# A hybrid attention and delta-rule layer on one core: fewer warm-up products ahead of the norm, a planner that counts a halved clock, and a new table of shifts

## The chip, the cores and the metric

The program runs on one core of one Trainium2 chip. The metric is device time in microseconds (us) of one execution; the time before is 871.31 us, the median of three runs. The engines are named as in the profile: PE is TensorE (its weight loads are PEld), DVE is VectorE, ACT is ScalarE, POOL is GpSimd, SP is SyncE, which issues nearly all transfers (its queue is SPq).

## What is computed

The reference is one layer over 512 latent tokens `x` of width 1024, with 256 context tokens `ctx`. Cut to what matters here:

```
mod = silu(c) @ w_ada + b_ada                       # and the same for c_ctx
h   = rms_norm(x,   g1) * (1 + sc1)  + sh1
hc  = rms_norm(ctx, g1) * (1 + csc1) + csh1
q, k, v, dq, dk, dv, dz, da, db, ga, gd = split(h @ w_in)     # and of hc @ w_in
y_attn = windowed attention with context keys, normed q and k, rotary positions, sinks
o_d    = gated delta rule in chunks of 64, forwards and backwards
y = sigmoid(ga) * (y_attn @ w_br_attn) + sigmoid(gd) * (y_d @ w_br_dn)
x = x + gt1 * (y @ w_out)
out = x + gt2 * (relu(norm(x) @ w_mlp1)**2 @ w_mlp2)
```

## The kernel before, in words

Features lie on the 128 partitions in eight groups of 128 (`kt` 0 to 7), tokens lie along the free axis. Every large product is made of three products in a rounded 32-bit format: the upper part of the weights by the upper and by the lower part of the features, and the lower part of the weights by the upper part of the features (`mm3`, L331, L333, L335). Upper parts are written by ACT, the lower ones by DVE. A weight tile takes one load, one ACT pass (L295) and one DVE pass (L300).

**The front.** PE begins with `NONES` = 30 products of a tile of ones by itself whose result nobody reads (L230). `norm_x` squares `x` in four pieces as they land (ACT L402, DVE L404 and L405) and sums them over the partitions with four products (L406); ACT then makes the inverse root of them (L185, a logarithm and an exponential). The condition vector goes through a SiLU on ACT (L185 on `c_cc`), which needs another table of functions than the logarithm, so a table load (L181) stands between the two. For each `kt`, `ada` brings two transfers of `w_ada` (512 KB each) and multiplies them in one group of eight L249; `columns` turns the result into columns (ACT L267, two PE L272, DVE L281 and L282); `features` and `features_c` make the upper and the lower part of `h` for `x` and for the context (DVE L339, ACT L340, DVE L341). Three weight tiles are worked on while this goes on: the one for `da` and `db` (`wab`) and two of `dk`. Unread products stand after the first columns (L276, eight of them) and after later ones (L434, fourteen in all). After them come the other tiles of `w_in` (`wh`, `wl`).

**The order of the work.** The order on each engine is not that of the code. `Lists` plays the whole program through with a table of costs (`Step.cost`): each instruction has a time in which its engine is taken and a time after which its result is there. Of the instructions that are ready on an engine, the one with the lowest rank goes next; the rank is the place in the code plus what the table `SHIFTS` adds for stretches of it. The order that comes out is then imposed on each engine. So a change of a cost or of a row of `SHIFTS` can move instructions anywhere in the program.

Further places that are spoken of: L566 in `qk_norm` sums the squares of `q` and `k` (ACT L563 makes the squares). L725 transposes attention weights, L894 and L1243 are small products of the delta rule, L1148 are products of the gates. At the end of the delta rule sixteen transposes (L1444) bring its result back to features on the partitions, DVE L1449 multiplies it by the gate, ACT L224 and DVE L225 split it, and the branch products (L331 again) read it. The output projection and the two MLP products follow.

Of the kernel before, what the change touches and what calls it, by code (L numbers as in the profile page):

```python
# [26 lines left out]
LEAD = 0  # L27
ATT = 32
NHALF = 3
NONES, NWAIT = 30, 8  # L30
AHEAD = 2
LATES = 3, 3
HPAUSE = 2
# [3 lines left out]
STICK = 50  # L37
NSKIP = 2
WARM = (0, 3, 3, 3, 2, 0, 0, 0)
NROWS = 2  # L40
ND1 = 3
NGD = 5
P = 128
# [8 lines left out]
HC = CH // 2  # L52
# [65 lines left out]
def tile_layer(ctx: ExitStack, tc: tile.TileContext, I: dict, out: bass.AP, dbg=None):  # L118
    nc = tc.nc
    V, A, G, PE = nc.vector, nc.scalar, nc.gpsimd, nc.tensor  # L120
# [17 lines left out]
    banks = Arena(lambda o, n: psum[:, o:o + n], 512, 8)  # L138
# [55 lines left out]
    ones = mats.tile([P, P], F32, name="ones")  # L194
# [33 lines left out]
    wb_ = banks.get(512, True)  # L228
# [166 lines left out]

    def norm_x():
        ss = bank()
        for i in range(4):
            b = alloc(1024)
            src = xs_[:, i * 1024:(i + 1) * 1024]  # L400
            n = 512 if i == 3 else 1024
            A.activation(b[:, :n], src[:, :n], AF.Square)  # L402
            if i == 3:
                V.tensor_tensor(b[:, n:], src[:, n:], src[:, n:], op=ALU.mult)  # L404
            V.tensor_tensor(b[:, :512], b[:, :512], b[:, 512:], op=ALU.add)  # L405
            PE.matmul(ss.ap, ones, b[:, :512], start=(i == 0), stop=(i == 3))  # L406
            b.free()
        act(rx, ss.ap, AF.Ln, bias=epsc, scale=1.0 / D)
        ss.free()
        return act(rx, rx, AF.Exp, scale=-0.5)  # L410
# [177 lines left out]
    own = [slice(0, 64), slice(64, 128)]  # L588
# [1163 lines left out]
class Step:  # L1752
# [39 lines left out]
    def cost(self):  # L1792

        n = self.cols
        if self.kind == "InstMatmult":
            if self.dtype.endswith("32r"):
                return (226 if n == 512 else max(60, 7 + .44 * n)), n * .44 + 175
            if self.dtype.endswith("16"):
                return 96, 240
            if self.whole:  # L1800
                return (110, 280) if self.ins.is_transpose else (max(62, 1.72 * n), max(62, 1.72 * n) + 170)
            return (142, 300) if self.tile[0] == P else (30 if self.tile[1] > HC else 19, 220)
        if self.kind == "InstStreamTranspose":
            return 1950, 2090
        if self.eng == "DVE":
            own = 67 + 1.04 * n + 60 * self.psum if n > 8 else 100
            return own, own + 85
        if self.eng == "Activation":
            own = 1290 if "Load" in self.kind else max(195, 36 + .893 * n) + 20 * self.psum
            return own, own + 130  # L1810
        return 550, 560
# [69 lines left out]
class Lists:  # L1881
# [27 lines left out]
    def run(self, rank):  # L1909

        n, after, gang, eng = self.n, self.after, self.gang, self.eng
        left, ready = list(self.left), [0.] * len(self.left)
        wait = [len(m) for m in self.members]
        free, links = [0., 0., 0., 0., 750.], [0., 0., 0., 0., 3200.]
        coming, here, out = [[] for _ in free], [[] for _ in free], []
        flight, whole, cold = [], True, False
        words, asked, begun, last = 0, {n: 0. for n in range(3)}, [0.] * n, 0.
        push, pop = heapq.heappush, heapq.heappop
        note = [SEEN[e] for e in self.ENGINES]

        def go(k):
            if k >= n:
                for x in after[k]:
                    ready[x] = max(ready[x], ready[k])
                    left[x] -= 1
                    if not left[x]:
                        go(x)
            elif gang[k] is None:
                push(coming[eng[k]], (ready[k], rank[k], k))
            else:  # L1930
                g = gang[k]
                wait[g] -= 1
                if not wait[g]:
                    t = max(ready[x] for x in self.members[g])
                    for x in self.members[g]:
                        push(coming[0], (t, rank[self.members[g][0]], x))

        for k in [k for k, m in enumerate(left) if not m]:
            go(k)
        for _ in range(n):  # L1940
            t, e = min((free[e] if here[e] else max(free[e], coming[e][0][0]), e) for e in range(5) if here[e] or coming[e])
            mine, come = here[e], coming[e]
            while come and come[0][0] <= t:
                push(mine, pop(come)[1:])
            k = mine[0][1]
            if e == 0 and self.whole[k] != whole:
                same = min((x for x in mine if self.whole[x[1]] == whole), default=None)
                if same and same[0] <= mine[0][0] + STICK:
                    k = same[1]
                    mine.remove(same)  # L1950
                    heapq.heapify(mine)
                else:
                    pop(mine)
            else:
                pop(mine)
            out.append(k)
            if self.dma[k]:
                if e == 4:
                    if len(flight) >= 8:
                        t = max(t, flight[-8])  # L1960
                    links[e] = end = max(t + (2400 if self.bytes[k] > 100000 else 1600), links[e]) + self.bytes[k] / 422
                    flight.append(end)
                    free[e] = t + 400
                else:
                    links[e] = end = max(t + 2400, links[e]) + self.bytes[k] / 159
                    free[e] = t + 900
            else:
                own, lag = self.cost[k]
                if e == 0:
                    words, had = words + self.words[k], words  # L1970
                    block = int(words / 256 + .63)
                    if block > int(had / 256 + .63):
                        asked[block] = max(t + 1100, links[4] - 500) + 1250
                    t = max(t, asked.get(int(had / 256 - .54), 0))
                    if self.whole[k] != whole:
                        t += 92 if whole else 130
                        cold = whole = self.whole[k]
                    elif cold and whole and self.wide[k]:
                        t, cold = t + 100, False
                end = t + lag  # L1980
                free[e] = t + own
            begun[k], last = t, max(last, end)
            for x in after[k]:
                if x >= n:
                    at = end + 40
                elif eng[x] == e and not self.dma[k]:
                    at = free[e] if e == 0 else end + 10
                else:
                    at = end + note[eng[x]]
                if at > ready[x]:  # L1990
                    ready[x] = at
                left[x] -= 1
                if not left[x]:
                    go(x)
        return out, begun, last


SHIFTS = (
# [12 lines left out]
)  # L2011


# [120 lines left out]
```

## Time and profile before

| what | value |
|---|---|
| median of three runs | 871.31 us (870.93 to 871.32) |
| profiled execution | 871.5 us, of which 869.7 us are its span |
| PE busy | 852.3 us, 98% of the span, 7544 products |
| DVE, ACT, POOL busy | 647.0, 498.4 and 26.1 us |
| granted TensorE clock, mean over the span | 1.00 |
| moved by DMA | 106.86 MB, 123 GB/s on average |
| SPq's transfers | 97.33 MB, 33.6% of the 16 DMA engines' span |

The span runs from the first to the last instruction; 1.8 us of the profiled execution lie around it. An engine counts as busy between the start and the modelled end of an instruction, and products overlap, so the time that one product takes from PE is read from the distance between starts. The first grant of the clock is not in the clock's column, which shows 1.00 from the start; what the clock was there is read from the distance of the products.

### The profile page before, as it was taken

The page shows a single profiled execution, that of the slowest core. Times are in us where ns is not written, and L with a number is a line of the kernel's source. Part 1 is how long each engine was busy: PE and PEld are TensorE (multiplying, and loading weights), DVE is VectorE, ACT ScalarE, POOL GpSimd, SP SyncE. Part 2 cuts the span into 40 slices and gives each one's busy share as a digit, 9 for nine tenths or more (in the row PEclk, how much of TensorE's full clock was granted, in tenths as well). Part 3 has the DMA queues.
Part 4 walks back from the last instruction along what each step waited for, and adds up shares of the span by engine and source line. Part 5 has one row for each costly group of instructions (what it writes and reads, how often), then busy time and mean ns, then how long its engine had stood idle before and what let it go on. Part 6 is the DMA issues. An engine that isn't in the chain of part 4 may idle for free.

```text
span 869.7 us, 17973 instructions
## 1 busy us (share of the span) xinstructions
PE 852.3 (98%) x7544; PEld 712.8 (82%) x7544; DVE 647.0 (74%) x1113; ACT 498.4 (57%) x882; POOL 26.1 (3%) x42
## 2 busy tenths in 40 slices
PE   9999999999999999899999999999999999999998
PEld 6688778877777778677778899888998899889986
DVE  4865899987779997867848969993876478648741
ACT  5567875487669886587754435552555256415620
POOL 0000001010000002000000000000000000000000
PEclk9999999999999999999999999999999999999999
DMA  9924465533121236733116744743412332342031
GB/s 365 352 72 98 88 134 122 120 76 70 38 38 31 68 131 212 243 99 100 40 54 220 264 144 131 249 139 121 146 33 74 122 140 70 97 128 92 26 121 49
DMA packets 31986, 106.86 MB, mean 123 GB/s; under 512 B 4001, under 2 KB 4513, under 8 KB 31905
## 3 DMA queue, kind: packets, MB, share of 16 engines
q1 hardware_dynamic: 29600, 97.33, 33.6%
q0 software_dynamic: 2304, 8.39, 6.2%
q8 instruction: 59, 0.97, 0.5%
q14 instruction: 23, 0.18, 0.1%
HBM read 103.61 MB, written 2.10 MB: 122 GB/s over the span
## 4 chain that ended last, share of the span: by engine, by line
PE 77%; DVE 9%; ACT 6%; DMA 6%; issue 2%; SPq 0%; ACTq 0%; DVEq 0%
PE banks L331 14%; PE banks L333 14%; PE banks L335 14%; PE banks L1612 14%; PE banks L1148 7%; DMA m<-in_wada 3%; PE banks L1243 3%; PE banks L1194 3%; ACT m L185 2%; PE banks L725 1%; DVE wl L300 1%; DMA wr<-in_win 1%; PE banks L781 1%; DVE m L511 1%; DMA wr<-in_wbr 1%
## 5 line engine op out<-in xcount | busy, mean ns | idle before, releaser
L331 PE MATMUL banks<-m,wh 128*128 128x512 f32 (+1 forms) x568 | 210.7, 374 | 2.2 <-ACT m L224 1.3
L333 PE MATMUL banks<-m,wh 128*128 128x512 f32 (+1 forms) x568 | 211.2, 372 | 0.0
L335 PE MATMUL banks<-m,wl 128*128 128x512 f32 (+1 forms) x568 | 209.9, 370 | 0.1
L295 ACT ACTIVATE wh<-wr 128x1024 fp32r<-128x1024 f32 (+1 forms) x92 | 90.4, 984 | 128.3 <-PE banks L333 82.7
L331 PEld LDWEIGHTS banks<-m,wh 128*128 128x128 f32 x568 | 107.0, 189 | 20.4 <-ACT m L224 1.5
L1612 PEld LDWEIGHTS banks<-m,m 128*128 128x128 f32 x1008 | 122.2, 192 | 0.7
L335 PEld LDWEIGHTS banks<-m,wl 128*128 128x128 f32 x568 | 106.9, 188 | 19.2 <-issue 1.0
L1612 PE MATMUL banks<-m,m 128*128 128x256 f32 x1008 | 122.4, 283 | 0.0
L333 PEld LDWEIGHTS banks<-m,wh 128*128 128x128 f32 x568 | 107.1, 188 | 18.1 <-issue 0.7
L224 ACT ACTIVATE m<-m 128x512 fp32r<-128x512 f32 (+2 forms) x118 | 82.4, 721 | 66.1 <-PE banks L1612 14.9
L1148 PE MATMUL banks<-m,wh 128*128 128x512 f32 x320 | 104.1, 402 | 1.8 <-ACT m L185 1.0
L225 DVE TENSOR_TENSOR m<-m,m 128x512 fp32r<-128x512 f32 (+2 forms) x118 | 92.3, 804 | 15.5 <-ACT m L224 13.9
L300 DVE TENSOR_TENSOR wl<-wr,wh 128x1024 fp32r<-128x1024 f32 (+1 forms) x76 | 84.3, 1109 | 17.1 <-ACT wh L295 14.6
L1739 DVE SCALAR_TENSOR_TENSOR m<-banks,modT,m 128x512 f32<-128x512 f32 x32 | 24.0, 749 | 65.0 <-PE banks L335 64.9
L1148 PEld LDWEIGHTS banks<-m,wh 128*128 128x128 f32 x320 | 58.6, 188 | 14.4 <-ACT m L185 1.4
L1148 PE MATMUL banks<-m,wl 128*128 128x512 f32 x160 | 63.7, 400 | 0.4 <-DVE wl L300 0.4
L331 PE MATMUL banks<-m,m 128*128 128x256 f32 (+1 forms) x136 | 45.5, 340 | 0.4 <-ACT m L295 0.3
L333 PE MATMUL banks<-m,m 128*128 128x256 f32 (+1 forms) x136 | 45.6, 342 | 0.1
L511 DVE SCALAR_TENSOR_TENSOR m<-m,m 128x1024 f32<-128x1024 f32 x32 | 39.1, 1222 | 8.4 <-DMA m<-in_wada 8.2
L335 PE MATMUL banks<-m,m 128*128 128x256 f32 (+1 forms) x120 | 40.2, 337 | 0.0
L1243 PEld LDWEIGHTS banks<-m,m 64*64 64x64 f32 x1600 | 26.7, 134 | 12.5 <-issue 4.3
L1148 PEld LDWEIGHTS banks<-m,wl 128*128 128x128 f32 x160 | 30.0, 188 | 7.3 <-DVE wl L300 1.1
(263 smaller groups left out, 1313.7 us busy)
## 6 DMA issues: line engine op xcount, KB each, us to landing
m<-in_wada SPq DMA_DIRECT2D x48, 512.0 KB, 4.8
wr<-in_wm SPq DMA_DIRECT2D x40, 512.0 KB, 3.6
wr<-in_win SPq DMA_DIRECT2D x38, 512.0 KB, 3.7
m<-in_wm SPq DMA_DIRECT2D x24, 512.0 KB, 3.7
wl<-in_win POOLq DMA_DIRECT2D x16, 512.0 KB, 5.8
m<-in_xT SPq DMA_DIRECT2D x8, 512.0 KB, 5.9
wr<-in_wbr SPq DMA_DIRECT2D x16, 256.0 KB, 2.7
wr<-in_wout SPq DMA_DIRECT2D x8, 512.0 KB, 4.4
```

Source lines behind the costliest of these rows:

```text
L224: A.activation(r32(hi), src, AF.Copy)
L225: (eng or V).tensor_tensor(r32(lo), src, hi, op=ALU.subtract)
L295: upper[0] = A.activation(r32(hi), raw, AF.Copy)
L300: V.tensor_tensor(r32(lo), raw, hi, op=ALU.subtract)
L331: PE.matmul(acc, w[0][:, k, :], xhi, start=(start and i == 0), stop=False)
L333: r = PE.matmul(acc, w[0][:, k, :], xlo, start=False, stop=(end and w[1] is None))
L335: r = PE.matmul(acc, w[1][:, k, :], xhi, start=False, stop=end)
L511: r = V.scalar_tensor_tensor(wa.ap, wa.ap, 0.5, scr_[0].ap, op0=ALU.mult, op1=ALU.mult, accum_out=modT[:, grp, j:j + 1])
L1148: PE.matmul(acc.ap, w[x][:, k, :], hx[k][y], start=(k == p == 0), stop=(k == KT - 1 and p == 2))
L1194: PE.matmul(pa.ap, w[x][:, j, :], r32(Q[y][:, :, j, :]), start=(j == p == 0), stop=(j == 3 and p == 2))
L1243: runs[n].append(PE.matmul(out_, w, x, start=True, stop=True).ins.name)
L1612: PE.matmul(dst, r32(self.w[w][i][:, k * P:(k + 1) * P]), xs7[x][k][j], start=(n == 0), stop=(n == 11))
```

## The change

The thirty unread products in front become sixteen. Inside `norm_x` four unread products follow the second of the four sums over squares and two follow the third (`XWARM`). In the planner a product that starts before 5500 ns takes twice its time (`COLD`), the costs of some kinds of products are changed, and an instruction that follows a transfer's issue on the same engine no longer waits for that transfer's end. The 60 rows of `SHIFTS` are replaced by 65 others.

```
-NONES, NWAIT = 30, 8
+NONES, NWAIT = 16, 8
+XWARM = (0, 4, 2, 0)
+COLD = 5500
...
         ss = bank()
+        wb_ = banks.get(512, True)
         for i in range(4):
...
-            PE.matmul(ss.ap, ones, b[:, :512], start=(i == 0), stop=(i == 3))
+            pe = PE.matmul(ss.ap, ones, b[:, :512], start=(i == 0), stop=(i == 3))
             b.free()
+            for _ in range(XWARM[i]):
+                follow(PE.matmul(wb_[:, :P], ones, ones, start=True, stop=True), pe)
+        wb_.free()
...
             if self.dtype.endswith("16"):
-                return 96, 240
+                return 80, 240
+            if self.whole and not self.ins.is_transpose:
+                return (max(224, 1.33 * n), max(224, 1.72 * n) + 170)
             if self.whole:
-                return (110, 280) if self.ins.is_transpose else (max(62, 1.72 * n), max(62, 1.72 * n) + 170)
-            return (142, 300) if self.tile[0] == P else (30 if self.tile[1] > HC else 19, 220)
+                return 110, 280
+            return (108, 400) if self.tile[0] == P else (30 if self.tile[1] > HC else 19, 220)
...
                 if e == 0:
+                    if t < COLD:
+                        own, lag = 2 * own, lag + own
...
                 elif eng[x] == e and not self.dma[k]:
                     at = free[e] if e == 0 else end + 10
+                elif eng[x] == e and self.dma[x]:
+                    at = free[e]
                 else:
...
 SHIFTS = (
-    (0, 2729, 2759, -37), (0, 7350, 8025, -10), (-1, 4917, 4924, 10), (0, 1436, 2436, 180), (-1, 5117, 5177, 30),
...
+    (-1, 5285, 5325, 5), (2, 2849, 2879, 1500), (0, 4631, 4781, 112), (-1, 7751, 7811, 1000), (-1, 2143, 2158, -90),
...
```

The rows of the table tell a reader nothing; what they do is seen in the order of the instructions. Lines of the changed kernel have other numbers (L148 becomes L150, L260 L262, L290 L292, L331 to L335 become L333 to L337, L566 L572, L894 L900, L918 and L919 L924 and L925, L1148 L1154, L1444 L1450), and buffers' numbers are some lower there. The small products of the delta rule keep their kinds; counted over the whole program, PE goes from whole-array products to products on a part of it or back 112 times before and 116 times now.

The first place is SP at the very start: `c_cc` is the condition vector, `c_prm` a table of small parameters, `in_wada` the weights of the modulation, `in_win` those of the input projection. Before:

```order
L260 DMA m_123<-in_xT 128x1024 x4
L148 DMA m_131<-in_wada 128x1024
L148 DMA m_137<-in_wada 128x1024
L148 DMA c_cc<-in_cc 128x16
L148 DMA c_prm<-in_prm 128x188
L309 DMA wr_143<-in_wab 128x512
L348 DMA m_124<-in_ctxT 128x1024 x2
L148 DMA m_153<-in_wada 128x1024
L148 DMA m_159<-in_wada 128x1024
L148 DMA m_221<-in_wada 128x1024
```

Now:

```order
L150 DMA c_cc<-in_cc 128x16
L150 DMA c_prm<-in_prm 128x188
L262 DMA m_109<-in_xT 128x1024 x4
L150 DMA m_117<-in_wada 128x1024
L150 DMA m_123<-in_wada 128x1024
L311 DMA wr_129<-in_wab 128x512
L350 DMA m_110<-in_ctxT 128x1024 x2
L150 DMA m_139<-in_wada 128x1024
L150 DMA m_145<-in_wada 128x1024
L292 DMA wr_153<-in_win 128x1024
L150 DMA m_213<-in_wada 128x1024
```

The two small transfers go ahead of `x`. The first tile of `w_in` goes ahead of the third pair of `w_ada` where it stood behind the first half of the fourth, and the second tile, which stood just ahead of the very last piece of `w_ada`, now stands ahead of the fifth pair.

The second place is PE between 104 and 114 us, in the middle of the first attention tiles (`m_1082` before and `m_1074` now hold the same squares, and so do `m_1188` and `m_1180`). Before:

```order
L894 MATMUL banks<-m_606 32x2x32 x4
L894 MATMUL banks<-m_608 32x2x32 x3
L566 MATMUL banks<-m_1082,c_bones 128x512
L333 MATMUL banks<-m_151,wh_817 128x512
L335 MATMUL banks<-m_151,wl_818 128x512
L331 MATMUL banks<-m_151,wh_817 128x512
```

Now:

```order
L333 MATMUL banks<-m_137,wh_809 128x512
L335 MATMUL banks<-m_137,wh_809 128x512
L337 MATMUL banks<-m_137,wl_810 128x512
L333 MATMUL banks<-m_137,wh_809 128x512
L572 MATMUL banks<-m_1074,c_bones 128x512
L335 MATMUL banks<-m_137,wh_809 128x512
L924 MATMUL banks<-m_1138,m_551 128x512
L925 MATMUL banks<-m_1138,m_551 128x512
```

Since the last sum of the kind before it, at 95 us, 28 wide (512) weight products came ahead of the first of the two, and now 46 and two more of L924 do. Counted from the same place, the second has 82 wide products ahead of it where it had 64, and the third, which follows right behind the second now, 82 where it had 90.

The third place is PE at 453 us, where the transposes of the delta rule's result (L1444, now L1450) stand between the last gate products (L1148, now L1154) and the first branch products. Before:

```order
L1148 MATMUL banks<-m_151,wl_5283 128x512
L1148 MATMUL banks<-m_151,wl_5407 128x512
L1148 MATMUL banks<-m_151,wh_5406 128x512 x2
L1148 MATMUL banks<-m_151,wl_5407 128x512
L1444 MATMUL banks<-c_ident,m_5369 128x128 x16
L331 MATMUL banks<-m_5362,wh_5439 128x512
```

Now:

```order
L1450 MATMUL banks<-c_ident,m_5361 128x128 x7
L1154 MATMUL banks<-m_137,wh_5398 128x512
L1450 MATMUL banks<-c_ident,m_5361 128x128
L1154 MATMUL banks<-m_137,wh_5398 128x512
L1154 MATMUL banks<-m_137,wl_5399 128x512
L1154 MATMUL banks<-m_137,wh_5398 128x512 x2
L1154 MATMUL banks<-m_137,wl_5399 128x512
L1450 MATMUL banks<-c_ident,m_5361 128x128 x5
L333 MATMUL banks<-m_5354,wh_5431 128x512
L1450 MATMUL banks<-c_ident,m_5361 128x128 x3
```

The first eight transposes went ahead of six gate products, and three of the last eight behind the first branch product. On ACT the first two splits (L224) of that result now stand ahead of the table load that they followed before.

## Rows read from the trace of the kernel before

**Rows 1.** Busy time in stretches of the span (stretch: its length, engines' busy us, clock, DMA).

```profile
44.00:72.00 28.00, 28.00 (x161) 24.51 (x160) 15.44 (x26) 19.22 (x26) 1.01 (x1) 1.00 0.28 79
72.00:460.00 388.00, 377.52 (x4675) 297.79 (x4674) 319.19 (x602) 277.45 (x576) 23.38 (x35) 1.00 0.38 99
460.00:869.70 409.70, 405.70 (x2391) 360.98 (x2389) 283.44 (x420) 175.91 (x238) 0.00 (x0) 1.00 0.38 123
```

**Rows 2.** Timeline of PE, first 13 us (start, us, what, idle before and releaser).

```profile
1.06 8.43 PE L230 MATMUL banks<-ones 128*128 128x128 f32 x60 [1.06 <-DVE ones L195]
9.33 3.60 PE L406 MATMUL banks<-m,ones 128*128 128x512 f32 x8
```

**Rows 3.** Busy time of L230 alone (PE, PEld), up to 4.16 us and after.

```profile
1.06:4.16 3.10, 3.10 (x14) 3.10 (x15) 1.00 0.74 243
4.16:9.33 5.17, 5.17 (x48) 5.14 (x46) 1.00 1.00 395
```

**Rows 4.** Timeline of ACT, 11.6 to 14.5 us.

```profile
11.62 0.22 ACT L185 ACTIVATE m<-c_cc 128x16 f32<-128x16 f32 x1 [2.11 <-DMA c_cc<-in_cc]
11.86 1.28 ACT L181 ACT_TABLE_LOAD   x1
...
13.69 0.67 ACT L185 ACTIVATE m<-banks,epsc 128x512 f32<-128x512 f32 x1
```

**Rows 5.** Timeline of DVE, the last piece of the squares of `x`.

```profile
10.13 0.69 DVE L405 TENSOR_TENSOR m<-m 128x512 f32<-128x512 f32 x1
```

**Rows 6.** Timeline of SP's queue, first 5 us.

```profile
0.75 1.81 SPq L260 DMA_DIRECT2D m<-in_xT  x4
...
3.56 0.44 SPq L148 DMA_DIRECT2D c_cc<-in_cc  x1
4.04 0.45 SPq L148 DMA_DIRECT2D c_prm<-in_prm  x1
```

**Rows 7.** DMA issues at 38.7, 16.2 and 26.0 us (KB each, us to landing).

```profile
c_nmask<-in_nmask SPq DMA_DIRECT2D x1, 32.0 KB, 2.5
...
m<-in_wada SPq DMA_DIRECT2D x1, 512.0 KB, 11.0
...
m<-in_wada SPq DMA_DIRECT2D x1, 512.0 KB, 9.9
```

**Rows 8.** Timeline of PE, the fifth and the eighth group of L249.

```profile
29.63 1.07 PE L249 MATMUL banks<-m,m 128*32 128x256 f32 x16
...
41.56 1.07 PE L249 MATMUL banks<-m,m 128*32 128x256 f32 x16
```

**Rows 9.** Busy time between those groups, and in a stretch of wide products alone.

```profile
29.63:41.56 11.93, 11.49 (x99) 8.21 (x99) 10.21 (x24) 7.81 (x15) 1.47 (x2) 1.00 0.92 345
53.20:57.06 3.86, 3.86 (x19) 3.19 (x17) 3.79 (x8) 3.72 (x6) 0.00 (x0) 1.00 0.01 2
```

**Rows 10.** Costliest groups, the narrow (256) products of L1612 (busy, mean ns, idle before).

```profile
L1612 PE MATMUL banks<-m,m 128*128 128x256 f32 x1008 | 122.4, 283 | 0.0
```

**Rows 11.** Timeline of PE, 102 to 115 us, the two sums L566.

```profile
103.84 1.12 PE L566 MATMUL banks<-m,c_bones 128*128 128x512 f32 x2 [0.32 <-ACT m L563]
...
113.84 1.13 PE L566 MATMUL banks<-m,c_bones 128*128 128x512 f32 x2 [0.65 <-ACT m L563]
```

**Rows 12.** Timeline of PE, 450 to 458 us, transposes and first branch products.

```profile
453.29 1.91 PE L1444 MATMUL banks<-c_ident,m 128*128 128x128 f32 x16
456.47 1.00 PE L331 MATMUL banks<-m,wh 128*128 128x512 f32 x3 [1.27 <-ACT m L224]
```

**Rows 13.** Timeline of ACT, 453 to 458 us.

```profile
453.89 0.59 ACT L185 ACTIVATE m<-banks 128x512 f32<-128x512 f32 x1
454.49 1.28 ACT L181 ACT_TABLE_LOAD   x1
455.79 1.67 ACT L224 ACTIVATE m<-m 128x512 fp32r<-128x512 f32 x3
```

**Rows 14.** Busy time from 140 to 240 us.

```profile
140.00:240.00 100.00, 96.73 (x802) 78.63 (x801) 83.39 (x163) 63.69 (x112) 9.00 (x12) 1.00 0.39 82
```

23 rows, old and new, of the table SHIFTS are left out of this document.

## The prediction

> **What bounds the kernel now.** I read the busy times by stretch first, since a share over the whole span mixes two regimes. From 460 us on PE is busy for 405.70 of 409.70 us, and what is missing is the transfer of the output at the end; from 44 to 72 us it is busy throughout [rows 1]. No order can gain there. What an order can give lies in two places: ahead of 44 us, where PE follows the weights of the modulation, and from 72 to 460 us, where PE stands idle for 388.00 - 377.52 = 10.5 us [rows 1]. Then the timeline of each engine over the front, to see who holds whom; then the issues of transfers; last, two places further on where PE waits and where the order changes. Because PE is full from 460 us to the end, whatever is gained or lost ahead of it arrives at the end whole.
>
> **How to read the front.** The thirty unread products take PE from 1.06 us to the first sum at 9.33 us, and the four sums take 3.60 us more, to 12.9 us [rows 2]. The first 3.1 us hold 14 of their 60 passes, 0.22 us each; the next 5.17 us hold the other 46, 0.11 us each [rows 3]. So the clock is at 1.2 GHz until about 4.16 us and at 2.4 after, although the clock's column shows 1.00. The last piece of the squares is ready at 10.13 + 0.69 = 10.8 us [rows 5], so the products in front do hold the sums up. But the inverse root begins only at 13.69 us: the SiLU of the condition vector has to wait for its transfer until 11.62 us, and the table load behind it takes ACT until 13.14 us [rows 4]. That transfer was issued fifth in SP's queue, at 3.56 us, behind 3 MB [rows 6].
>
> **The change, part by part.**
>
> *Sixteen products in place of thirty, and six between the sums.* The same 14 passes are slow, 18 of the 32 fast, so PE is free at 4.16 + 18 x 0.112 = 6.2 us in place of 9.3. Each sum then waits for its square. The six new products (12 passes, 1.3 us) lie in those waits. By itself this moves the last sum's end from 12.9 to what the squares allow, 10.8 + 0.9 = 11.7 us.
>
> *Two small transfers ahead of x.* They take SP 0.44 + 0.45 us [rows 6], so `x` starts 0.9 us later, and all that follows it in the queue by about 0.5, since the two no longer stand between later ones. The last square is then ready near 11.7 and the last sum done at 12.6 us: 0.3 us ahead of before. In return the SiLU's input is there early: the shortest landing in the front is 2.5 us after the issue [rows 7], 3.3 us here, so the table load is done by 5 us and leaves the root's path. The root starts near 12.7 in place of 13.69, a gain of 1.0 us for the first features if no weight holds them.
>
> *The weights of the modulation and the order of PE.* This decides what the front is worth. The fifth group of L249 starts at 29.63, the eighth and last at 41.56 us [rows 8], while its weights, issued at 26.0 us with 9.9 us to landing, are there at 35.9 [rows 7]. PE reaches them 5.7 us late because products of the early tiles stand ahead of them. A wide product takes 3.86 / 17 = 0.227 us of PE (17 loads in a stretch of nothing else), a narrow one 122.4 / 1008 = 0.12 [rows 9, 10]. Between the two groups the order has 13 wide and 21 narrow products before, and 8 and 19 now, with all else equal: 5 x 0.227 + 2 x 0.12 = 1.4 us less, so 11.93 - 1.4 = 10.5 us if waits stay, and 0.44 us less if none does, the time that PE is idle there [rows 9]. Where does the fifth group start now? Its weights landed at 16.2 + 11.0 = 27.2 us [rows 7], 2.4 us before it ran. Now one more `in_win` tile (512 KB, 1.3 us at the 395 GB/s of [rows 3]) stands ahead of them and the queue is 0.5 us late: 29.0. If PE follows at once the group starts at 29.0; if the 2.4 us were those of features, at 31.4. I take 30.2, the middle, since the features start about 1 us earlier but the third pair of weights, behind that tile too, lands some 1.8 us later. The last group then starts at 30.2 + 10.5 - 0.2 = 40.5, 1.1 us earlier (earliest 29.0 + 10.1 = 39.1, latest 31.4 + 10.5 = 41.9). Ahead of it PE has done 24 wide and 21 narrow early products where it had 22 and 28: 0.4 us less. **Net: 0.7 us gained at 44 us, between -0.7 and +2.1.** Since the second `in_win` tile now stands ahead of the fifth pair, work is at hand for every wait, which speaks for the upper half: I take **1.0**. What is late next is the third and fourth tile of `w_in`, moved behind the constants; by their place in the queue I estimate that they land near 41 and 43 us, and by the count of products ahead that PE asks for the first of them after 46, so nothing.
>
> *The two sums L566.* PE waits 0.32 and 0.65 us there for ACT's squares [rows 11]. Both sums now stand behind 20 and 18 more wide products (4.5 and 4.1 us), which need nothing from ACT. **1.0 us**, between 0 and 1.0; what stands behind the sums is a rival below.
>
> *The end of the delta rule.* PE runs all sixteen transposes and then waits 1.27 us for ACT's split [rows 12]. The split starts at 455.79, right behind a table load of 1.28 us that starts at 454.49 [rows 13]. Now the first eight transposes go some 1.5 us earlier, ahead of six gate products (6 x 0.227), and the first two splits go ahead of the table load. By the order and the durations I estimate DVE's product ready by 454.4 and the split by 455.1, where PE has run out of other work at 455.0. **1.2 us**, between 0 and 1.3. The table load that moves behind two splits holds only what comes after them.
>
> *All other moved instructions.* PE's other waits between 72 and 460 us come to 10.5 - 1.0 - 1.3 = 8.2 us [rows 1, 11, 12]. The new costs and shifts reorder all of them, and no row says which go and which come. I take 0, between +4.1 and -4.1, half of them. Four more passages between whole and partial products (116, not 112) lie inside that. POOL's queue keeps its order.
>
> Sum: 1.0 + 1.0 + 1.2 = 3.2 us. The profiled execution, 871.5 us with 1.8 around its span, would take 868.3; it stands 0.2 above the median, so against the median 871.3 - 3.2 = **868.1 us**.
>
> **The clock, weighed.** The rows show one moment of the rise, 4.16 us [rows 3], and thirty products cover any other up to 9.3 us; sixteen cover less. The Trainium skill, "TensorE: Matmul & The Clock Gate", Part 1, says that the budget for warming up is one of time and not of products, and that the moment wanders from run to run of one kernel. By the first half the cut costs nothing, as the rows have it too; by the second a later rise would leave sums at half speed, which one run cannot show.
>
> **The rivals.**
>
> *A. The other waits shrink too.* For it: the same edit frees two of them, and the changed costs lie nearer to what the trace shows (a 128-wide pass of ones at 0.11 us, a halved clock ahead of 4.16 us [rows 3]). Against: eight small waits with as many causes. Half of 8.2 us: 868.1 - 4.1 = 864.0.
>
> *B. The front gives nothing.* PE reaches the last group no earlier, because the later `x` and the later third and fifth pairs eat up what the order saves; of the two waits further on, one comes back behind other work. 871.3 - 1.1 = 870.2.
>
> *C. Slower: the norm's chain.* The first sum L566 is put off by 20 x 0.227 = 4.5 us, and behind it stand ACT's root, DVE's products, and all scores of the attention. Between 140 and 240 us PE has only 3.3 us idle and DVE 16.6 us [rows 14]; if the scores are what PE lives on there, the 4.5 us come back as waits. With the 1.0 and 1.2 us of the other places kept: 871.3 + 4.5 - 2.2 = 873.6. It decides from the point where PE's idle time in that stage grows by more than 2 us. Against it: the third sum comes 8 wide products earlier, and DVE has room.
>
> *D. The clock rises late or falls.* If PE's clock were still at 1.2 GHz when the sums run, they take 3.60 us more, of which some 1.5 us are hidden in waits for squares: 2.1 us on the root, less the 1.0 gained there: +1.1 on the front in place of -1.0; with the other 2.2 kept, 871.3 + 1.1 - 2.2 = 870.2, and 872.4 without them.
>
> *E. The change does not act* (the orders above show that it moves the instructions): 871.3.
>
> **How the numbers follow.** Forecast 0.45 (866.9, the best ends of its terms, to 869.6; their worst ends, 872.0, are B and C), A 0.15, B 0.20, C 0.12, D 0.06, E 0.02. Here 0.2%, about 1.7 us, is what a measurement can tell from no change. Faster: the forecast, A, and a quarter of B, 0.65. Slower: C, 0.12, and a little of D, 0.13 in all. Same: the rest, 0.22. The range takes A's 864.0 as its low end and 872.7 as its high one, which holds B, D and E; outside are C and the far half of A, 0.19.
>
> **What would show it.** Right: L230 ends near 6.2 us, and 14 of its passes are slow; the SiLU ends by 4 us and no table load stands ahead of the root, which starts near 12.7; the eighth group of L249 starts between 39 and 42 us; the wait ahead of the first branch product is under 0.3 us; no wait for squares ahead of the two sums. Wrong: the eighth group at 42 us or later (B), PE idle for over 5 us between 140 and 240 us (C), passes of the sums at twice 0.43 us (D), or PE idle for about 4 us instead of 8 at the other places (A).

## The result: slower, and where the trace puts it

| what | before | the change |
|---|---|---|
| median | 871.32 us (870.93 to 872.71, 5 runs) | 874.93 us (873.83 to 877.04, 5 runs) |
| ratio | | 1.0043 (1.0030 to 1.0056) |
| profiled execution, its span | 871.5, 869.7 us | 875.6, 873.8 us |
| granted clock, mean over the span | 1.00 | 0.998 in four runs, 0.994 in one |

868.1 us was forecast, with 864.0 to 872.7 around it; the change is 0.43% slower, to which I had given 0.13.

The busy times by stretch, in the columns of [rows 1]:

```profile
44.00:72.00 28.00, 28.00 (x161) 24.48 (x161) 17.00 (x27) 19.37 (x26) 0.02 (x1) 1.00 0.21 62
72.00:460.00 388.00, 377.74 (x4667) 298.56 (x4666) 316.31 (x597) 275.40 (x575) 24.33 (x36) 1.00 0.38 98
460.00:873.80 413.80, 408.73 (x2402) 363.08 (x2400) 286.89 (x425) 179.53 (x242) 0.00 (x0) 1.00 0.38 125
```

From 72 to 460 us PE stands idle for 10.3 us, where it was 10.5. Ahead of 460 us nothing seems won or lost, and yet the span is 4.1 us longer. So busy time does not tell it. I compared the two traces by the work that remains: each product counts with what it takes in a full stretch (a wide one 0.227 us, a narrow one 0.12, the small ones the mean distance of their kind, unread ones nothing), and at a given place the **lag** is the difference between the times at which both kernels have the same work left. Where the two orders differ it is good to some 0.5 us; a change of it over a stretch of one order is good to 0.1.

| time in before, us | 60 | 150 | 262 | 318 | 357 | 448 | 470 | 700 | 730 | 860 |
|---|---|---|---|---|---|---|---|---|---|---|
| lag of the change, us | 0.4 | -0.4 | -1.4 | 0.5 | 4.4 | 4.1 | 2.6 | 2.8 | 3.9 | 4.0 |

The change is 1.4 us ahead at 262 us. It loses 1.9 us by 318 and 3.9 more by 357, wins 1.5 at the branch products and loses 1.1 near 712 us, in the stretch in which I had said that no order can gain or lose.

**The front.** PE's timeline and the busy time of L232, which was L230 (answering to [rows 2, 3]):

```profile
1.07 6.66 PE L232 MATMUL banks<-ones 128*128 128x128 f32 x32 [1.07 <-DVE ones L197]
8.14 2.38 PE L409 MATMUL banks<-m,ones 128*128 128x512 f32 x4 [0.41 <-DVE m L408]
10.35 1.05 PE L412 MATMUL banks<-ones 128*128 128x128 f32 x8
11.24 1.02 PE L409 MATMUL banks<-m,ones 128*128 128x512 f32 x2
12.10 0.61 PE L412 MATMUL banks<-ones 128*128 128x128 f32 x4
12.55 1.02 PE L409 MATMUL banks<-m,ones 128*128 128x512 f32 x2
```

```profile
1.07:7.02 5.95, 5.95 (x28) 5.95 (x29) 1.00 0.78 234
7.02:8.10 1.08, 0.71 (x6) 0.52 (x5) 1.00 1.04 417
```

The clock rose at 7.02 us and not at 4.16: 28 passes took 5.95 us, 0.21 each. It cost nothing, because the first sum has to wait for its square until 8.14 us anyway. ACT's timeline, for [rows 4], then a line of ACT's before that [rows 4] leave out, and the groups of L251 (L249 before) on PE, for [rows 8]:

```profile
2.43 0.22 ACT L187 ACTIVATE m<-c_cc 128x16 f32<-128x16 f32 x1 [0.40 <-DMA c_cc<-in_cc]
...
13.21 0.63 ACT L315 ACTIVATE m<-wr 128x512 fp32r<-128x512 f32 x1 [2.53 <-DMA wr<-in_wab]
13.75 0.67 ACT L187 ACTIVATE m<-banks,epsc 128x512 f32<-128x512 f32 x1
```

```profile
13.15 0.63 ACT L313 ACTIVATE m<-wr 128x512 fp32r<-128x512 f32 x1
```

```profile
30.65 1.07 PE L251 MATMUL banks<-m,m 128*32 128x256 f32 x16
...
41.35 1.07 PE L251 MATMUL banks<-m,m 128*32 128x256 f32 x16
```

The SiLU is done by 2.7 us, and yet the root starts at 13.75 us where it started at 13.69. Two things hold it there. The last square is ready at 12.0 us (DVE, 11.31 + 0.69), but its sum begins at 12.55, behind the third sum and the unread products L412, and ends at 13.57. And ACT has the upper part of `wab` (L315) ahead of the root, whose transfer lands at 13.2 us; that pass stood ahead of the root before, too. The fifth and the eighth group come at 30.65 and 41.35 us.

**From 270 to 460 us.** PE's waits there (waiting line, what for: us in total, times, longest), the longest wait for "issue" before, and the busy time of PE now in pieces around the longest (stretch: length, busy, clock, DMA):

```profile
PE banks L1010 <- issue: 2.1, 1, 2.1
PE banks L1154 <- ACT wh L297: 1.8, 1, 1.8
PE banks L1037 <- ACT m L187: 1.0, 1, 1.0
PE banks L1200 <- ACT m L1042: 0.7, 1, 0.7
```

```profile
PE banks L1004 <- issue: 1.2, 1, 1.2
```

```profile
338.60:341.30 2.70, 1.97 (x158) 1.00 0.73 262
341.30:343.40 2.10, 0.02 (x1) 1.00 0.41 135
343.40:345.00 1.60, 1.58 (x119) 0.98 0.96 346
345.00:348.20 3.20, 3.20 (x9) 0.50 0.96 270
348.20:351.00 2.80, 2.80 (x13) 0.97 0.39 155
```

In 2.7 us PE runs 157 passes of small 32x32 products without a wide one between them (the end of one first stage, L999 and L1000, a whole first stage, and the start of a second one, L1009 and L1010), and then stands for 2.1 us for nothing that the page shows ("issue"). Behind that the clock is granted at half from 344.94 to 348.35 us, which costs 1.7 us, half of that time. Before, 35, 20 and 4 wide products stood between the stages, the longest such wait was 1.18 us, and the clock stayed whole.

The wait is one for PE's own code, which the queue q8 brings (more on it with e5). In the change a packet of q8 runs from 341.24 to 342.17 us, and PE goes on at 343.42. All 18 waits for issue of over 0.6 us in the 16 profiles end so: 1.25 to 1.62 us after the end of a packet of q8. What differs most is how early the packet starts: 0.1 us ahead of the wait here, 1.6 us ahead of it before (347.70 and 349.26 us).

**The branch products**, for [rows 12, 13], PE and then ACT:

```profile
458.39 0.71 PE L1450 MATMUL banks<-c_ident,m 128*128 128x128 f32 x5
458.90 0.50 PE L333 MATMUL banks<-m,wh 128*128 128x512 f32 x1
```

```profile
458.21 0.63 ACT L226 ACTIVATE m<-m 128x512 fp32r<-128x512 f32 x1 [1.00 <-DVE m L1455]
```

No wait is left there, as forecast. **Near 712 us**, DVE and then PE:

```profile
703.49 0.69 DVE L1595 TENSOR_TENSOR m<-m,m 128x512 f32<-128x512 f32 x1 [1.23 <-DMA m<-in_wm]
```

```profile
715.31 1.94 PE L1618 MATMUL banks<-m,m 128*128 128x256 f32 x14 [0.92 <-DVE m L227]
```

DVE waits for a tile of `in_wm`, and twelve microseconds later PE waits for DVE. Before, neither waited.

### The profile page after: what moved, and what is told of

It is laid out like the page before. It is cut to its first block, busy times and chain, and to the rows that moved or that the text cites. A ratio compares the mean times of both kernels' runs of the same rounds, so it can differ in the third digit from the quotient of the medians.

```text
span 873.8 us, 17942 instructions
## 1 busy us (share of the span) xinstructions
PE 855.1 (98%) x7528; PEld 714.4 (82%) x7528; DVE 648.1 (74%) x1113; ACT 498.7 (57%) x882; POOL 26.0 (3%) x42
## 4 chain that ended last, share of the span: by engine, by line
PE 81%; ACT 7%; DVE 6%; DMA 3%; issue 2%; SPq 0%; DVEq 0%; ACTq 0%
PE banks L333 15%; PE banks L335 15%; PE banks L337 15%; PE banks L1618 12%; PE banks L1154 9%; PE banks L1249 3%; PE banks L1200 2%; PE banks L731 2%; ACT m L187 2%; DVE m L341 1%; DMA m<-in_wada 1%; PE banks L787 1%; DVE m L343 1%; ACT m L1042 1%; DMA m<-in_wm 1%
## 5 line engine op out<-in xcount | busy, mean ns | idle before, releaser
L333 PE MATMUL banks<-m,wh 128*128 128x512 f32 (+1 forms) x568 | 211.4, 375 | 0.0
L335 PE MATMUL banks<-m,wh 128*128 128x512 f32 (+1 forms) x568 | 210.0, 370 | 0.0
L337 PE MATMUL banks<-m,wl 128*128 128x512 f32 (+1 forms) x568 | 209.2, 370 | 0.0
L1618 PE MATMUL banks<-m,m 128*128 128x256 f32 x1008 | 126.2, 283 | 0.9 <-DVE m L227 0.9
L333 PEld LDWEIGHTS banks<-m,wh 128*128 128x128 f32 x568 | 107.0, 189 | 18.7 <-ACT wh L297 0.7
L337 PEld LDWEIGHTS banks<-m,wl 128*128 128x128 f32 x568 | 106.9, 188 | 18.2
L335 PEld LDWEIGHTS banks<-m,wh 128*128 128x128 f32 x568 | 107.1, 189 | 17.5 <-issue 0.5
L1154 PE MATMUL banks<-m,wh 128*128 128x512 f32 x320 | 105.9, 406 | 2.5 <-ACT wh L297 1.8
L1154 PEld LDWEIGHTS banks<-m,wh 128*128 128x128 f32 x320 | 59.6, 191 | 16.0 <-ACT wh L297 2.3
L1154 PE MATMUL banks<-m,wl 128*128 128x512 f32 x160 | 64.2, 404 | 0.0
L335 PE MATMUL banks<-m,m 128*128 128x256 f32 (+1 forms) x136 | 45.8, 343 | 0.6 <-DVE m L343 0.6
L333 PE MATMUL banks<-m,m 128*128 128x512 f32 (+1 forms) x136 | 45.2, 340 | 0.4 <-ACT m L342 0.3
L337 PE MATMUL banks<-m,m 128*128 128x512 f32 (+1 forms) x120 | 40.3, 335 | 0.0
L1154 PEld LDWEIGHTS banks<-m,wl 128*128 128x128 f32 x160 | 30.4, 190 | 6.8
```

Of the source, the lines that this page charges most:

```text
L333: PE.matmul(acc, w[0][:, k, :], xhi, start=(start and i == 0), stop=False)
L335: r = PE.matmul(acc, w[0][:, k, :], xlo, start=False, stop=(end and w[1] is None))
L337: r = PE.matmul(acc, w[1][:, k, :], xhi, start=False, stop=end)
L1154: PE.matmul(acc.ap, w[x][:, k, :], hx[k][y], start=(k == p == 0), stop=(k == KT - 1 and p == 2))
L1618: PE.matmul(dst, r32(self.w[w][i][:, k * P:(k + 1) * P]), xs7[x][k][j], start=(n == 0), stop=(n == 11))
```

## The experiments

Two devices serve most of them. The first keeps both planners in one kernel, the changed costs with the new shifts and the old costs with the old ones (their places moved by the eight products that are missing), and takes the order from the one up to a time of its plan and from the other behind it:

```
+PHASES = ((False, 257000), (True, 1000000000.0))        # (old planner?, until)
...
+    for old, until in PHASES:
+        out, begun = plans[old]
+        last = max((i for i, k in enumerate(out) if begun[k] < until), default=-1)
+        for k in out[:last + 1]:
+            if k not in done:
+                done.add(k)
+                order.append(k)
```

The program, its sixteen and its six products are those of the change in all of them. The second adds eight unread products, in `columns(0)`, behind the first group of L251, where PE waits for ACT; to the planner they cost nothing:

```
+            for _ in range(PADS):                               # 8
+                follow(PE.matmul(wb_[:, :P], ones, ones, start=True, stop=True), ends[0])
```

Each ratio is to runs of the kernel before made beside it (medians 871.6 to 871.8 us).

| run | order, by time in us | eight more | median | ratio to before (95%) |
|---|---|---|---|---|
| e1 | before's | no | 873.03 | 1.0014 (1.0004 to 1.0024) |
| e2 | change's to 270, before's | no | 872.57 | 1.0015 (1.0004 to 1.0026) |
| e3 | before's to 270, change's | no | 875.96 | 1.0046 (1.0033 to 1.0059) |
| e4 | change's, sixteen wide products moved | no | 874.55 | 1.0031 (1.0019 to 1.0044) |
| e5 | before's | yes | 871.67 | 0.9996 (0.9986 to 1.0005) |
| e6 | change's | yes | 875.26 | 1.0039 (1.0027 to 1.0052) |
| e7 | before's to 44, change's to 270, before's to 445, change's to 690, before's | no | 871.94 | 1.0001 (0.9992 to 1.0010) |
| e8 | as e7 | yes | 870.43 | 0.9985 (0.9975 to 0.9995) |
| e9, e10 | change's, loads of the front moved | no | 885.02, 885.44 | 1.0154, 1.0161 |
| e11 | change's, before's from 322 to 362 | no | 875.98 | 1.0042 (1.0027 to 1.0058) |
| e12 | as e8, with 234 in place of 270 | yes | 869.71 | 0.9976 (0.9964 to 0.9987) |
| e13 | change's, before's from 270 to 362 | no | 870.83 | 0.9992 (0.9984 to 1.0001) |
| e14 | change's, before's from 270 to 322 | no | 875.28 | 1.0045 (1.0029 to 1.0061) |

**The front alone (e1).**

> Only the products in front are changed (16 in place of 30, six between the sums); costs, rules and shifts are those of before, so every engine's order is that of before apart from these products. Theory T (the loss sits in the new order further on): the front gives or takes less than 0.6 us, time 870.7 to 871.9. Rival F (the late rise of the clock in front, 27 slow passes in place of 14, costs the time): 873 or more, with the lag already there at 44 us.

The lag is -0.8 to -0.9 us from 44 to 330 us: the shorter front is worth that. But the whole is 1.4 us slower, mostly by 1.9 us lost near 370 us and 1.0 near 712, with an order that is the one of before to the last instruction. Neither theory has that. At 366 us PE waits 2.62 us for an upper part of weights, and the clock falls at the end of that wait; at 712 us it waits as the change does.

**Each half (e2, e3).**

> The order of the change up to about 270 us of the span, the order of before behind that. Theory T: the change is 1.4 us ahead at 270 us and loses only behind it, so 871.3 - 1.4 = 869.9, and the clock stays whole at 340 to 350 us. Rival F: 873 or more.

> The order of before up to about 270 us, the order of the change behind that. Theory T: all losses without the gain of the first part: 871.3 + 5.3 = 876.6, with a wait for issue of about 2 us and a halved clock of about 3 us near 345 us. Rival F: 871 to 872.

The order behind 270 us carries the loss: the lag of e3 goes from -1.0 at 262 us to 0.9 at 318 and 4.8 at 357, that of e2 from -1.2 only to -0.5 and -0.7. That is T, but e2 ends 1.0 us behind before where 1.4 us ahead was expected, and 1.6 us of that are lost near 712 us, with the order of before in that place.

**The code, not the order (e5, e6).** PE's instructions come in pieces of 16 KB: queue q8 moved 59 of them in the change, for 7528 passes and as many loads, so 255 instructions each. Eight products less, of two loads and two passes each, are 32 instructions less, and every later piece ends 32 instructions further on in the program, which in a stretch of wide products is 16 of them, 3.6 us. In before a fetch lies at 690.2 us, 3.7 us ahead of the issue of the `in_wm` tiles at 693.8; in e1 it falls on that issue. The transfers from 693 to 697 us in e1:

```profile
q8 instruction: 1, 0.02, 1.6%
...
m<-in_wm SPq DMA_DIRECT2D x2, 512.0 KB, 4.9
```

> As the run with the front alone changed, with eight more unread products behind the first group of eight L251, where PE stands idle for 1.5 us: PE has as many instructions as before again, so the 16 KB pieces in which its code is fetched end at the same places of the program as before. Theory C (the shorter code moves the fetches onto transfers that matter): the fetch near 690 us lies ahead of the in_wm transfers again, DVE does not wait for them at 701 us, PE does not wait at 712 us (0.8 us there), and the time is 870.6 to 871.2. Rival R (the losses come from the earlier start or from chance, not from the code): the wait at 712 us stays, 872.5 to 873.0.

> The changed kernel with the same eight products, its order otherwise untouched. Theory C: the wait at 714 us goes (1.2 us), and the wait for issue near 341 us, 2.1 us in the change, gets another length, since the piece of code ends eight products away from there: 872.0 to 874.0. Rival R: both waits as in the change, 874.9 or a little more.

With the eight products the fetch is back ahead of the tiles. In e5 it lies from 689 to 692 us, the first of these two views; from 693 to 697 us, the second, q8 has none, and the tiles need 4.1 us to landing:

```profile
q8 instruction: 1, 0.02, 1.9%
```

```profile
q1 hardware_dynamic: 135, 0.52, 38.2%
q14 instruction: 1, 0.01, 0.5%
issues: line engine op xcount, KB each, median us to landing
m<-in_wm SPq DMA_DIRECT2D x2, 512.0 KB, 4.1
```

The wait at 712 us is gone in e5, e6, e8 and e12, the four with the eight products. The eleven without them, the change, e1 to e4, e7, e9 to e11, e13 and e14, all have a fetch within 0.4 us of that issue, and ten of them lose 0.4 to 1.6 us there; e14 has the fetch and not the wait. An earlier start does not make the wait: e12 is 1.5 us ahead of before at 700 us and has none. So C holds for this place: e1 loses 1.0 us there and e5 nothing, e7 0.4 and e8 nothing. The rest of what separates the medians, 1.4 us from e1 to e5 and 1.5 from e7 to e8, is not shown to come from this place. The mean granted clock goes the same way, 0.9968 to 0.9988 and 0.9965 to 0.9987 over eleven executions each, which by an estimate (the difference times 871 us) is 1.7 and 1.9 us; why eight products move it stays open. For e6 as a whole C fails: the wait for issue near 341 us became 2.4 us and in the profile the clock still fell, twice, and the median is 875.26 us where 872.0 to 874.0 was expected. The Trainium skill, "Runtime: NRT & Kernel Launch", Instruction fetch mechanics, says that the code comes in blocks of 16 KiB over a queue of its own and that the fetch is hidden by the pace at which instructions go out; the trace agrees with the first, and PE's waits for issue of 0.9 to 2.4 us in stretches of small products, in every profile here, speak against the second, as does the packet of q8 that ends shortly ahead of the end of each.

**Wide products between the small ones (e4).**

```
+    gates = [k for k in sequence if 3237 <= k < 3253 and steps[k].eng == "PE"]
+    sequence = [k for k in sequence if k not in gates]
+    at = sequence.index(3155)                    # the first product of the second stage
+    for k in sequence[:at] + gates + sequence[at:]:
```

> The changed kernel, with sixteen wide gate products (3.6 us) moved from behind the second stage of the small 32x32 products at 341 us to between its first and second stage; nothing else differs. Theory T: PE's 2.1 us wait for issue goes, and the clock that fell behind it stays whole (1.7 us more): 874.9 - 3.8 = 871.1. Rival G: the wait for instructions goes but the clock falls all the same: 872.8. Rival H: the wait only moves to the next stretch of small products: 874 to 875.

H: the wait for issue only moved, to five passes ahead of the end of the second stage, and was 2.34 us. One gap is not enough. In the profile the clock fell behind it. Yet five of the ten executions have a mean clock of 0.999 or 1.00 and took 873.1 to 874.6 us, and two of e6's five at 1.00 took 874.1 and 874.9, so the clock is a part of the loss and not all of it.

**Which stretch (e11, e13, e14).**

> The changed kernel with the order of before between about 322 and 362 us alone, where the wait for issue (2.1 us) and the halved clock (1.7 us) stand. Theory T (the order in this stretch makes them): 874.9 - 3.0 to 3.8 = 871.1 to 871.9, a wait for issue of about 1.1 us there. Rival P (what comes ahead of the stretch sets where the pieces of code end, and so the wait): a wait of 1.9 to 2.4 us stays, 874 to 875.

> The changed kernel with the order of before from about 270 to 362 us, all else as in the change. Theory T (the new order in this stretch makes the waits at 277 and 283 us, the longer wait for issue at 341 us and, behind it, the halved clock): 874.9 - 2.0 - 2.5 to 3.9 = 869.0 to 870.4, plus up to 0.8 us of waits at the two passages; no execution-wide fall of the clock at 345 us. Rival P (the new order behind 362 us or the shorter code brings the waits back elsewhere): 873 or more.

> The changed kernel with the order of before from about 270 to 322 us alone. Theory T: the waits at 277 and 283 us go, the one for issue (1.9 to 2.4 us) and the clock's fall stay: 874.9 - 2.0 = 872.9, plus up to 0.8 us of waits at the passages. Rival Q (what comes ahead of 322 us also makes the wait for issue): that wait falls to about 1.1 us and the clock stays whole: 869 to 871.

e11 did not settle it: the wait for issue fell to 0.86 us, as T has it, but at the passage PE waited 1.25 us, in two waits, for a transposition of DVE's, and the clock fell there. Its two executions at the full clock took 872.9 and 874.0 us. e13 and e14 differ in the order of the 40 us from 322 to 362 alone, and by 4.5 us. e14 has the wait and the fall (PE by stretches):

```profile
337.40:340.10 2.70, 1.96 (x158) 1.00 0.72 282
340.10:342.20 2.10, 0.01 (x2) 1.00 0.46 135
342.20:343.80 1.60, 1.60 (x119) 0.97 0.80 264
343.80:347.10 3.30, 3.30 (x10) 0.50 0.98 361
```

e13, over the same products:

```profile
338.00:352.00 14.00, 13.06 (x423) 1.00 0.77 249
```

Here PE is idle for 0.94 us, all of it the wait for issue. Six of twelve executions of e13 have a mean clock of 1.00, none of six of e14 and none of five of the change. The mean clocks over the executions, 0.9992 and 0.9950, differ by what an estimate (the difference times 872 us) puts at 3.7 us, and the waits for issue differ by 1.2. So most of the 4.5 us is the clock; a part of it falls behind the stretch, for in e14's profile a second halved stretch begins at 374.4 us. T holds for this stretch, and Q falls. The other half is smaller than I had it: the waits at 277 and 283 us go in e14, its lag at 318 us is -0.8 where the change has 0.5, and its median is not lower for it; two halved stretches instead of one, in its profile, ate that.

**The loads of the front (e9, e10).** In these, SP's first 8 and first 27 transfers have the order of before.

> The changed kernel with the two small transfers behind x and the first pair of w_ada again, as before; the rest of SP's order and all other engines as in the change. Read at 44 us against before: the change stood 0.3 to 1.0 us behind there, the order of before with the same sixteen and six products 0.8 to 1.0 us ahead. Theory U (the later x costs it): ahead of before at 44 us. Theory V (the moved weights) or W (PE's order): 0.3 to 1.0 behind, as in the change. The whole: 874.0 under U, 875 under V and W.

> As that run, with the first 27 transfers of SP all in the order of before (x, w_ada and in_win), the other engines as in the change. Theory V: ahead of before by 0.5 to 1.0 us at 44 us, the whole 873.8. Theory W: behind by 0.3 us or more, 875.

Both failed as a test. ACT has the SiLU ahead of the squares in the change's order, so with `c_cc` behind `x` the squares start at 13.46 and 12.95 us, and the front costs 8.9 and 11.5 us. They show only that the loads and ACT's order can't be taken apart.

**The good stretches together (e7, e8, e12).**

> Five stretches: the order of before up to about 44 us (front gain 0.9), that of the change to 270 us (1.85 ahead from L566 and the scores), that of before to 445 us, that of the change to 690 us (1.4 at the branch products), that of before to the end; no extra products. Theory T: the gains add up, 871.6 - 4.1 = 867.5, and with the wait at 712 us that the shorter code brings (theory C) 868.5. Rival S (a gain ahead of 340 us is eaten by later waits, because the weights there come from transfers that do not come earlier): 870 to 871.5.

> The same five stretches with the eight extra products. Theories T and C: 867.5 to 868.0, a microsecond under the run without them and no wait at 712 us. Rival R: as the run without them or up to 0.3 us slower. Rival S: 870 to 871.5.

> The five stretches with the eight extra products, with the passage from the change's order back to that of before at about 234 us in place of 270 us, since PE waited 1.7 us at that passage where it waits 1.0 before. If that wait comes from the passage: 0.7 us better than the run with the later passage, 869.7; if the weights' transfers near 366 us set the time, the same 870.4.

e8's median is 1.5 us under e7's, with the eight products as the only difference; their profiled executions are as long as each other, 869.8 and 869.6 us of span, and only 0.4 us of it is seen at 712 us (above). Both fall short of 867.5: the passage at 270 us makes a wait of 1.7 us (1.0 before), and near 370 us e8 loses 1.8 us to a wait of 2.45 us for weights and the fall of the clock behind it. With the earlier passage that wait is 0.95 us again, and e12 at 869.71 us (869.14 to 869.98) is faster than before and than the change.

## Why the prediction was wrong

- **The step that failed** is "All other moved instructions ... I take 0, between +4.1 and -4.1, half of them". Between 262 and 357 us they cost 5.8 us (lag from -1.4 to 4.4). I had bounded them by the waits that were there. The new order made a wait that no wait of before bounds, 2.1 us for code, and behind it the clock was granted at half, which no term of the sum had. e13 against e14 puts 4.5 us on the order of the 40 us around it, more than the bound for all eight waits together, and most of that is clock.
- **"No order can gain there"**, of the time from 460 us on, failed by 1.1 us. I had not counted that fewer products are also less code: with before's order, e1 loses 1.0 us there and e5 nothing.
- **The front, +1.0.** As a gain of fewer products it was right: -0.7 to -0.9 us at 40 us in e1, e3 and e7, which have before's order there; with the eight products back it is -0.4 and -0.5 in e12 and e8, and only -0.1 in e5. The way there was wrong: the root did not start at 12.7 but at 13.75 us. The six new products were to lie in waits, but they stand between a square and its sum: the last sum began 0.55 us after its square and ended at 13.57 us, not at 12.6. Without `wab` the root could have started some 0.1 us earlier and no more (in e9, where ACT is free, it starts 0.04 us after the last sum). I had also overlooked the pass of `wab`, which stood ahead of the root before as well, and `c_cc` was issued seventh and not fifth; the 3 MB ahead of it are right. The eighth group came at 41.35 us, in the range given (39.1 to 41.9) and not at 40.5. e7 has before's order to 44 us and the change's behind it, and has the lags of the change at 60, 150 and 262 us (0.4, -0.4, -1.3), so the changed front of the profiled execution is worth as much as the old one with sixteen products. In the other profiles with that front it stood from 0.2 us better (e14) to 2.1 us worse (e11, whose clock was granted at half from 22.1 to 25.5 us), so one profile does not settle what it is worth.
- **L566, +1.0.** Both waits went. What came of it is smaller: e12, with the change's order from 44 to 234 us and before's on both sides, goes from -0.4 at 40 us to -0.9 at 330, 0.5 us for the whole stretch.
- **The branch products, +1.2.** Right: no wait is left, and the lag falls by 1.5 us, in e3 by 1.4 and in e12 by 1.5.
- **The rivals.** C had the sign and the size and the wrong place: from 140 to 240 us PE's idle time fell from 3.3 to 2.8 us. D had the clock, in the front, where the late rise cost nothing. The Trainium skill, "TensorE: Matmul & The Clock Gate", Part 1, has that moment wander from run to run, and the profiles agree: by the passes of L232 it lies at 4.13 us in e3, 4.19 in e4, 5.85 in e2, 6.71 in e1. B and A spoke of waits alone. The fall of the clock near 345 us was in the price of none of them.

## What to carry to other kernels

A planner's table can only be judged stretch by stretch: this change was 1.4 us ahead by 262 us, won 1.5 at the branch products and lost six in the hundred microseconds between, and its best parts, pieced together, beat both kernels. Look for long runs of small products on PE, since there it can outrun its own code: a stage of 128 passes is 256 instructions, a whole piece, and PE was through with it in 1.3 us in the change, while a piece took 0.9 us to come and PE 1.25 more to go on. A wait of some two microseconds can cost as much again in clock. The planner reckons with the pieces of code (`words` and `asked` in `Lists.run`) and still gave this order; whether its figures for them are off was not tried. And a product that nobody reads is still code: before it is taken out or put in, see which transfers the fetches will fall on, or keep the number of instructions.

## What the runs showed that I had not expected

- Eight products fewer at the start moved a wait of 0.8 to 1.0 us into a place 700 us later (e1 against e5).
- Between 270 and 460 us the halved clock lasted 3.4 us each time. It came at or behind waits of PE of 2.10 us (the change, e14), 2.34 (e4), 2.40 (e6, e9), 2.45 (e8) and 2.62 us (e1), but also behind 1.08 us (e11), 1.36 (e12), 1.61 (e7) and 1.66 or 1.67 (e3, e10, and second falls of e6, e10 and e14), while e3 kept its clock behind 1.90 us, the change behind 1.78 and e2 and e13 behind 1.72. What decides it there stays open.
- The wait for issue depends on the order around it: 0.9 to 1.6 us with before's order from 322 to 362 us (before, e1, e2, e5, e7, e8, e11, e12, e13), 1.7 to 2.4 us with the change's (the change, e3, e4, e6, e9, e10, e14). How many wide products it takes between the small ones, and where, was not tried beyond e4.
